# GLA heads six weight blocks apart, v kept in the output's tile, the merge gate in q's and k's, relu and chunk bias on ScalarE

## Chip, cores and metric

One NeuronCore of a Trainium2 chip. The metric is the device time of one execution in microseconds. Before the change: median 1881.58 us of 3 runs (1880.73 to 1882.31).

## The reference, cut to what matters

An encoder block on 256 tokens of 2048 channels in float32: gated linear attention (GLA, 4 heads, both directions) beside a Hyena branch, merged by sigmoid gates, projected, layer norm, then a squared-ReLU MLP and a second norm. The change lies in the GLA part. For each head and direction:

```python
log_a = log_sigmoid(a @ wa2 + ba) / 16            # decay per key channel
b = cumsum(log_a within chunks of 64 tokens)
q_in, k_in = q * exp(b), k * exp(-b)
k_end = k * exp(b[last of chunk] - b)
scores = tril(q_in @ k_in.T)                      # inside a chunk
o = scores @ v + q_in @ state                     # state: sum of k_end.T @ v of earlier chunks, decayed
```

The two directions' outputs are added, normed per head, scaled by a gain and silu(r), and later projected with `w_gla_o`. `sigmoid(g1)`, the first merge gate, then multiplies that projection.

## The kernel before

**Weights.** Every projection is a sequence of blocks of 128 x 2048 floats. `fetch` (L89) loads one block into `raw` (three buffers, SP queue) and splits it in two halves of 1024 columns: ScalarE rounds to `whi` (L81), VectorE takes the remainder to `wlo` (L82); three buffers each. TensorE multiplies high and low parts in separate matmuls and sums in PSUM. A token block (r, v, w_out, the second MLP matrix: `token_products`, L183) has 24 matmuls of 512 columns; a channel block (`channel_pair`, L157: q, k, g1, u, go, ...) has 16 of 512 columns (L142) and 16 of 256 (L146), after which ScalarE copies the low half out (L154) and VectorE adds the high half (L155).

**Order.** `later(d, fn)` (L110) queues a piece of side work; `pump()` (L114) runs once per weight block and calls the pieces that are due d pumps after they were queued; `drain()` calls what is left. The tile scheduler then lays out each engine's instruction order, and puts in the semaphores, from priorities and buffers. Each engine executes its own order strictly in sequence.

**The GLA stage.** The r blocks end with the Hyena filters' last side work, whose results leave by `Td` stores on the POOL queue (L415). Then 16 token blocks for v (four per head) and 16 channel blocks for g1 (two per pair, eight pairs). Beside them, per head h:

- `gla_gates` (L477): z by 4 matmuls (L495); per direction |z| on ScalarE (L499), min(z, 0) on VectorE (L500), Exp and Ln (L501, L502), the difference (L503), a scan per chunk giving b (L508/L510); three exponentials of b: exp(b) (L514), exp(-b) (L515), and for the third the differences to the chunk's last value on VectorE (L518) and their Exp (L520); then products with q and k on VectorE (L522 to L547). b is kept as 16 times the logarithm and the factor 1/16 sits in the exponentials' scale.
- `gla_scores` (L552): score matmuls (L569) from these products, copies, a masked copy, and a split into `sth`, `stl`.
- `gla_out` (L581): 12 matmuls with v (L289 to L291) into two PSUM banks `o`; per bank a square with its sum (L593), the inverse root by Ln and Exp (L212, L213) and small VectorE ops, the product y (L595); then 8 transposes (`yt`, L602) and the split into `yT` (called `yg` in the trace).

For each head the loop (L609) queues gates (0 pumps), scores (3), runs the head's four v blocks, splits the v sums into `vh`, `vl` (high priority, one buffer each), and queues the output (1 pump). Behind the loop `m_sb` (L622) takes two new tiles in the memory of q and k, `channel_pair` writes the g1 sums to them, and at the end of the stage one sigmoid per pair (L636) turns them into the gate. The scheduler may place a sigmoid as soon as its pair is written. Sigmoid and Exp/Ln use different activation tables; a table load is put in wherever ScalarE's order changes from one to the other.

## Time and profile before

| | us |
|---|---|
| median of 3 runs | 1881.58 |
| profiled execution | 1878.99 |
| its span, first to last instruction | 1877.2 |
| TensorE (PE) busy | 1859.6 |
| VectorE (DVE) busy | 1317.7 |
| ScalarE (ACT) busy | 940.8 |
| v blocks, first to last matmul starts | 253.2 to 359.3 |
| g1 blocks | 359.5 to 472.7 |

An engine's busy time counts its instructions from start to end. Matmuls overlap: each row's 0.39 us is longer than the slot it takes in the stream, so costs are read from one start to the next. A row of the timeline has start, duration, engine, line, operation, output<-input, shapes, count, and in brackets the idle time before it with what ended it. A row of waits has the total, the number of times and the longest.

### The profile page before, as it was taken

Reading aid. Unit: us, or ns where it says so; the run is one execution under the profiler, and the core shown is the slowest. Engines: PE = TensorE matmul, PEld = TensorE weight load, DVE = VectorE, ACT = ScalarE, POOL = GpSimd, SP = SyncE. Lnnn points to the kernel's source line nnn. Section 1 sums busy time; section 2 is a strip of 40 time slices with the busy share of each in tenths; the row PEclk is TensorE's granted clock in tenths of the full one; section 3 lists DMA queues with packets and bytes.
Section 4 is the critical chain, followed back from the end, with each engine's and each line's share of the span. In section 5 each row is a group of like instructions: output and inputs, shape, how many; then the busy total and the mean of one; then the engine's idle time right before and its main releaser. Section 6 shows DMA issues by size and latency. Waiting matters only on the chain.

```text
span 1877.2 us, 25196 instructions
## 1 busy us (share of the span) xinstructions
PE 1859.6 (99%) x9948; PEld 1599.3 (85%) x9948; DVE 1317.7 (70%) x1711; ACT 940.8 (50%) x1278; POOL 30.8 (2%) x61
## 2 busy tenths in 40 slices
PE   9999999989999999999999999999999999999998
PEld 7888888878888888888888889888888888888887
DVE  6788878875799999888656667666555655565556
ACT  5555557675555555555544445444434443444332
POOL 1000000000000000000000000000000000000000
PEclk9999999999999999999999999999999999999999
DMA  8567664426555555555555654555555555555553
GB/s 295 208 243 279 227 256 154 180 90 211 185 200 206 197 198 195 201 208 208 213 189 193 259 214 178 201 182 198 182 199 185 199 181 201 187 195 182 199 189 125
DMA packets 60550, 375.07 MB, mean 200 GB/s; under 512 B 6832, under 2 KB 9552, under 8 KB 21008
## 3 DMA queue, kind: packets, MB, share of 16 engines
q1 hardware_dynamic: 47376, 324.03, 48.0%
q0 software_dynamic: 6288, 30.16, 4.3%
q10 hardware_dynamic: 6768, 19.27, 2.8%
q8 instruction: 78, 1.28, 0.3%
q14 instruction: 40, 0.33, 0.0%
HBM read 356.66 MB, written 16.78 MB: 199 GB/s over the span
## 4 chain that ended last, share of the span: by engine, by line
PE 88%; issue 7%; DVE 3%; ACT 1%; DMA 1%; POOL 0%; SPq 0%; DVEq 0%; POOLq 0%; ACTq 0%
PE f L142 12%; PE f L146 7%; PE g L142 6%; PE w L196 6%; PE w L194 6%; PE w L195 6%; PE uz L142 3%; PE ux L142 3%; PE go L142 3%; PE uv L142 3%; PE ho L142 3%; PE g L146 3%; PE ho L146 2%; PE go L146 2%; PE ux L146 2%
## 5 line engine op out<-in xcount | busy, mean ns | idle before, releaser
L82 DVE TENSOR_TENSOR wlo<-raw,whi 128x1024 fp32r<-128x1024 f32 (+2 forms) x603 | 728.6, 1211 | 273.7 <-ACT whi L81 271.0
L81 ACT CAST whi<-raw 128x1024 fp32r<-128x1024 f32 (+2 forms) x603 | 625.0, 1039 | 337.8 <-PE w L196 188.2
L142 PE MATMUL f<-hT,whi 128*128 128x512 f32 (+1 forms) x1048 | 247.6, 387 | 0.0
L142 PEld LDWEIGHTS f<-hT,whi 128*128 128x128 f32 x1048 | 190.9, 189 | 35.5
L195 PE MATMUL w<-wlo,f 128*128 128x512 f32 x480 | 186.7, 389 | 0.0
L196 PE MATMUL w<-whi,f 128*128 128x512 f32 x480 | 186.7, 389 | 0.0
L194 PE MATMUL w<-whi,f 128*128 128x512 f32 x480 | 167.4, 389 | 0.0
L146 PEld LDWEIGHTS f<-hT,wlo 128*128 128x128 f32 x1048 | 134.1, 191 | 4.8
L146 PE MATMUL f<-hT,wlo 128*128 128x256 f32 (+1 forms) x1048 | 135.8, 282 | 0.0
L142 PE MATMUL g<-xT,whi 128*128 128x512 f32 x512 | 124.3, 392 | 3.7 <-DVE vl L82 3.7
L142 PEld LDWEIGHTS g<-xT,whi 128*128 128x128 f32 x512 | 93.7, 188 | 22.1 <-DVE vl L82 4.1
L154 ACT ACTIVATE f_l<-f 128x256 f32<-128x256 f32 x64 | 24.6, 384 | 163.2 <-PE f L142 163.2
L194 PEld LDWEIGHTS w<-whi,f 128*128 128x128 f32 x480 | 90.1, 188 | 18.7
L196 PEld LDWEIGHTS w<-whi,f 128*128 128x128 f32 x480 | 90.1, 188 | 18.7
L195 PEld LDWEIGHTS w<-wlo,f 128*128 128x128 f32 x480 | 90.1, 188 | 18.7
L155 DVE SCALAR_TENSOR_TENSOR f_s<-f,f_l 128x256 f32<-128x256 f32 x64 | 27.2, 425 | 108.8 <-ACT f_l L154 108.7
L146 PEld LDWEIGHTS g<-xT,wlo 128*128 128x128 f32 x512 | 66.0, 191 | 2.6
L146 PE MATMUL g<-xT,wlo 128*128 128x256 f32 x512 | 67.5, 283 | 0.0
L142 PE MATMUL ux<-xT,whi 128*128 128x512 f32 x256 | 64.6, 393 | 0.0
L142 PE MATMUL uz<-xT,whi 128*128 128x512 f32 x256 | 64.5, 393 | 0.0
L142 PE MATMUL go<-yg,whi 128*128 128x512 f32 x256 | 63.6, 392 | 0.0
L142 PE MATMUL uv<-xT,whi 128*128 128x512 f32 x256 | 63.6, 391 | 0.0
(353 smaller groups left out, 3017.5 us busy)
## 6 DMA issues: line engine op xcount, KB each, us to landing
raw<-wblk SPq DMA_DIRECT2D x302, 1024.0 KB, 4.8
Td<-T POOLq DMA_DIRECT2D x16, 768.0 KB, 5.2
Tl<-Td POOLq DMA_DIRECT2D x16, 768.0 KB, 4.6
w<-w4s ACTq DMA_DIRECT2D x16, 512.0 KB, 5.2
zr<-ln_rows ACTq DMA_DIRECT2D x4, 1024.0 KB, 11.1
raw<-wblk SPq DMA_DIRECT2D x11, 256.0 KB, 6.9
dec<-decay_in ACTq DMA_DIRECT2D x8, 256.0 KB, 4.8
yd<-yo POOLq DMA_DIRECT2D x8, 256.0 KB, 4.0
```

The costliest lines, as they stand in the source:

```text
L81: nc.scalar.copy(hi, src)
L82: nc.vector.tensor_tensor(lo, src, hi.bitcast(F32), op=ALU.subtract)
L142: MM(ps[:, :, ts], hi[:, js], act[:, kt, :, ts], start=(kt == 0 and opens), stop=(kt == KT - 1))
L146: MM(ps[:, 0, ts], lo[:, js], act[:, kt, 0, ts], start=False, stop=False)
L154: nc.scalar.activation(low, ps[:, 1], AF.Copy, scale=scale)
L155: nc.vector.scalar_tensor_tensor(dst, ps[:, 0], scale, low, op0=ALU.mult, op1=ALU.add)
L194: MM(pss[tb], sh, wh, start=(kt == 0), stop=False)
L195: MM(pss[tb], sh, wl, start=False, stop=False)
L196: MM(pss[tb], sl, wh, start=False, stop=(kt == KT - 1))
```

## The change

- v: `vh`, `vl` are no tiles of their own. Head h's high and low parts lie in `yT[:, 4h:4h+4]`, the quarter of the output tile that head h's own output is written to later.
- Spacing: all side work of the four heads is queued before the first v block: gates at pump 6h, scores at 6h+4, output at 6h+7 (before: gates at 4h, scores at 4h+3, output at 4h+5).
- Merge gate: `m_sb` is `q_sb` and `k_sb` themselves, no new tiles.
- min(z, 0) on VectorE becomes relu(-(z + bias)/16) on ScalarE, with a bias tile `nba_sb` made once by a 128x16 VectorE op; the difference of L503 becomes a scalar_tensor_tensor that brings in the factor 1/16. b is now the logarithm itself, and exp(b), exp(-b) need no 1/16.
- The third exponential: the VectorE difference over 512 columns and one Exp of 512 become, per direction, six Exps of 64 columns with the chunk's last value of b as per-partition bias. The fourth chunk of each, which nothing reads, is left out.

```diff
+    nba_sb = gp.tile([P, 2, 8], F32, tag="nba", name="nba_sb")
+    nc.vector.tensor_scalar(nba_sb, ba_sb, -1.0 / TAU, None, op0=ALU.mult)
...
                     nc.scalar.activation(a[:, c, :], pzc, AF.Abs, bias=bias)
-                    nc.vector.tensor_scalar(m[:, c, :], pzc, bias, 0.0, op0=ALU.add, op1=ALU.min)
+                    nc.scalar.activation(m[:, c, :], pzc, AF.Relu, scale=-1.0 / TAU,
+                                         bias=nba_sb[:, d, 2 * h + c:2 * h + c + 1])
                 nc.scalar.activation(a, a, AF.Exp, scale=-1.0)
                 nc.scalar.activation(a, a, AF.Ln, bias=ones_sb)
-                nc.vector.tensor_tensor(m, m, a, op=ALU.subtract)
+                nc.vector.scalar_tensor_tensor(m, a, -1.0 / TAU, m, op0=ALU.mult, op1=ALU.subtract)
...
-                nc.scalar.activation(e1, b, AF.Exp, scale=1.0 / TAU)
-                nc.scalar.activation(e2, b, AF.Exp, scale=-1.0 / TAU)
+                nc.scalar.activation(e1, b, AF.Exp)
+                nc.scalar.activation(e2, b, AF.Exp, scale=-1.0)
                 last = 63 if d == 0 else 0
-                b4 = ch4(b)
-                nc.vector.tensor_tensor(
-                    ch4(e3), b4[:, :, :, last:last + 1].broadcast_to([P, 2, 4, 64]), b4, op=ALU.subtract)
-                nc.scalar.activation(e3, e3, AF.Exp, scale=1.0 / TAU)
+                for c in range(2):
+                    for i in ((0, 1, 2) if d == 0 else (1, 2, 3)):
+                        t64 = slice(64 * i, 64 * i + 64)
+                        nc.scalar.activation(e3[:, c, t64], b[:, c, t64], AF.Exp, scale=-1.0,
+                                             bias=b[:, c, 64 * i + last:64 * i + last + 1])
...
     for h in range(HEADS):
-        later(0, gla_gates(h))
-        later(3, gla_scores(h))
-        vh = gp.tile([P, NT, 512], F32R, tag="vh", name=f"vh{h}")
-        vl = gp.tile([P, NT, 512], F32R, tag="vl", name=f"vl{h}")
+        later(6 * h, gla_gates(h))
+        later(6 * h + 4, gla_scores(h))
+        later(6 * h + 7, gla_out(h))
+    for h in range(HEADS):
+        v2 = yT[:, 4 * h:4 * h + 4].rearrange("p k i l -> p (k i l)").rearrange("p (i t d) -> p i t d", i=2, t=NT)
+        vh, vl = v2[:, 0], v2[:, 1]
         pss = token_group(xT, f"v{h}")
...
         v_sb[h] = (vh, vl)
-        later(1, gla_out(h))
...
-    m_sb = [
-        qp.tile([P, 8, L], F32, tag="q", name="m0"),
-        qp.tile([P, 8, L], F32, tag="k", name="m1"),
-    ]
+    m_sb = [q_sb, k_sb]
```

More of the change, by code (lines that the diff above doesn't have):

```diff
@@ L493, in run @@
                     pzc = pz[:, c * L:(c + 1) * L]
-                    bias = ba_sb[:, d, 2 * h + c:2 * h + c + 1]
                     MM(pzc, ws[:, d * L + c * P:d * L + (c + 1) * P], as_sb, start=True, stop=True)
```

## The prediction

> **What bounds the kernel now.** I read the page first, then the busy time by stretches, then what TensorE waited for, then the timeline of the one stretch with a hole in it. From the page:

> ```profile
> span 1877.2 us, 25196 instructions
> PE 1859.6 (99%) x9948; PEld 1599.3 (85%) x9948; DVE 1317.7 (70%) x1711; ACT 940.8 (50%) x1278; POOL 30.8 (2%) x61
> ```

> TensorE is busy in all but 17.6 us of the span, and this change alters none of its matmuls. So only holes in TensorE's stream can be won, and only where the change acts: from the v blocks to the g1 blocks, 253 to 473 us. Busy time by stretches (window, its length, then PE, PEld, DVE, ACT, POOL):

> ```profile
> 282.00:329.00 47.00, 46.74 (x234) 38.77 (x233) 41.15 (x78) 34.23 (x63) 0.00 (x0) 1.00 0.44 152
> 329.00:376.00 47.00, 46.70 (x278) 39.75 (x276) 38.14 (x73) 28.91 (x55) 0.00 (x0) 1.00 0.49 178
> 376.00:423.00 47.00, 41.05 (x244) 35.16 (x245) 33.07 (x74) 35.58 (x66) 0.53 (x1) 1.00 0.26 91
> ```

> The holes are 0.26, 0.30 and 5.95 us: nearly all where head 2's end, head 3 and the last v splits meet. What TensorE waited for (total, times, longest), of its twelve rows those that lie in this stretch:

> ```profile
> PE g L142 <- DVE vl L82: 3.7, 1, 3.7
> PE o L289 <- ACT sth L81: 1.2, 1, 1.2
> PE yt L602 <- DVE y L595: 1.1, 1, 1.1
> PE z L495 <- DVE yg L82: 0.4, 1, 0.4
> ```

> Together 6.4. The largest in the timeline:

> ```profile
> 380.39 0.39 PE L291 MATMUL o<-vh,stl 128*128 128x512 f32 x1
> 384.45 2.11 PE L142 MATMUL g<-xT,whi 128*128 128x512 f32 x8 [3.67 <-DVE vl L82]
> ```

> The reader is to see a chain: v of head 3 could not be split while `vh`/`vl`, one buffer each, still held head 2's v; head 2's output matmuls end at 380.39; only then come the splits that empty v's PSUM banks, which the next gate block needs. The row counts the hole from the modelled end of a 0.39 matmul. Start to start, 4.06 passed where a matmul's slot is about 0.23 (worked out below), so 3.83 was lost: 0.16 more than the row. For four holes that makes 6.4 + 0.6 = **7.0**.

> **The change part by part.**

> *Places and spacing.* v of each head gets its own quarter of `yT`, so its split waits for no earlier head: the 3.83 goes. Scores now come four pumps behind the gates, outputs three behind the scores. In the built kernel's instruction order head 2's score matmuls stand a gate block and more ahead of its output matmuls (before: next to them), and head 3's z matmuls stand later. The 1.2 and the 0.4 go. The merge sums write `q_sb`/`k_sb` pair by pair behind the head that reads that pair: no wait that I can find. All weights, stores and loads keep their order on the SP and POOL queues. From uv on all engines' orders are those of before, but for one f matmul moved by a place; nothing is gained or lost there.

> *VectorE loses* two groups:

> ```profile
> L500 DVE TENSOR_SCALAR gm<-z,ba_sb 128x256 f32<-128x256 f32 x16 | 7.2, 480 | 0.1
> L518 DVE TENSOR_TENSOR e<-gb 128x512 f32<-128x512 f32 x8 | 5.5, 688 | 0.0
> ```

> That is 12.7 us less, over a stretch where it leaves TensorE waiting 0.26 + 0.30. I count half of that, 0.3, as won. One op comes in: the 128x16 scaled bias, which lies in memory that the last filter store still reads:

> ```profile
> 268.63 0.53 POOL L415 DMA_DIRECT2D Td<-T  x1 [10.26 <-DVE T L413]
> 273.22 0.34 ACTq L472 DMA_DIRECT2D scan_sb<-scan_in  x1
> 273.87 1.23 DVE L82 TENSOR_TENSOR wlo<-raw,whi 128x1024 fp32r<-128x1024 f32 x1 [1.50 <-ACT whi L81]
> ```

> The store had landed by 273.22, since the scan load waits for it too. The new op stands ahead of the split at 273.87, where VectorE sat idle 1.50. Cost: nothing. Were the store later, the weight splits behind the op would be late by as much.

> *ScalarE gains* per head four relus, and twelve 64-column exponentials for two of 512. Their prices, from rows where it runs without a gap (each cost is start to next start):

> ```profile
> 377.58 0.84 ACT L499 ACTIVATE ga<-z,ba_sb 128x256 f32<-128x256 f32 x2
> 378.31 1.15 ACT L501 ACTIVATE ga<-ga 128x512 f32<-128x512 f32 x2
> 379.35 1.33 ACT L502 ACTIVATE ga<-ga,ones_sb 128x512 f32<-128x512 f32 x2
> 380.57 0.59 ACT L593 ACTIVATE y<-o 128x512 f32<-128x512 f32 x1
> 381.05 0.20 ACT L593 ACTIVATION_READ_ACCUMULATOR y<-o 128x1 f32 x1
> 381.14 1.07 ACT L81 CAST vh<-v 128x512 fp32r<-128x512 f32 x2
> ...
> 382.67 0.32 ACT L212 ACTIVATE rq_t<-ss,eps_sb 128x1 f32<-128x1 f32 x1
> 382.86 0.65 ACT L514 ACTIVATE e<-gb 128x512 f32<-128x512 f32 x1
> 383.37 0.65 ACT L515 ACTIVATE e<-gb 128x512 f32<-128x512 f32 x1
> ```

> Abs with a per-partition bias, and so a relu: 0.365. Exp 0.52, Ln 0.61, a square with its sum 0.57, one column with such a bias 0.19, the exponentials of b 0.51. No row has 64 columns with a bias. Below it lies the one column, 0.19; above it the 256 columns, 0.365. I take 0.24, near the lower end, as 64 of 256 columns would. That is 4 x 0.365 + 12 x 0.24 - 2 x 0.51 = 3.3 us more per head. In the first two windows ScalarE has 12.8 and 18.1 us to spare, so heads 0 to 2 hide it. I laid those orders out with the same prices, and the tightest split comes some 0.6 ahead of its matmul. Without that cover each 0.1 is a 0.1 lost.

> *Head 3 and the table loads.* The built order has fifteen table loads, before eleven. Head 3's gates now run when the first g1 pair is done, and its sigmoid stands between them: loads for the sigmoid, for Exp, for Ln and for the Exp of head 2's norm come in a row. The price:

> ```profile
> 418.36 0.20 ACT L213 ACTIVATE rq_y<-rq_t 128x1 f32<-128x1 f32 x1
> 418.47 0.37 ACT L154 ACTIVATE g_l<-g 128x256 f32<-128x256 f32 x1
> 418.74 1.04 ACT L81 CAST whi<-raw 128x1024 fp32r<-128x1024 f32 x1
> 419.79 1.28 ACT L636 ACT_TABLE_LOAD   x1
> 421.09 0.63 ACT L636 ACTIVATE m<-m 128x512 f32<-128x512 f32 x1
> 421.62 1.03 ACT L81 CAST whi<-raw 128x1024 fp32r<-128x1024 f32 x1
> 422.56 1.06 ACT L81 CAST yg<-yt 128x512 fp32r<-128x512 f32 x2
> ```

> A weight split costs 0.94 in a row of others, but ahead of a load it is waited out (1.05), and 1.30 later the next starts: a load costs 1.40. Sigmoid 0.53, low half 0.27, one-column Exp 0.11.

> [...]

> Now ScalarE's work from the end of g1's first pair to the high half of block 54 (first half of `g1_2_1`), in the new order: 3 low halves 0.81, 5 splits 4.70, 8 abs/relu 2.92, 4 loads 5.60, sigmoid 0.53, 2 Exp 1.04, 2 Ln 1.22, 2 squares 1.14, 2 + 2 one-column 0.60, 4 exponentials 2.06, 12 short ones 2.88: **23.5**, with 0.3 for start and last tail 23.8. TensorE's work in the same stretch: 4 z, 3 blocks, 12 output matmuls, 2 transposes (0.11 each, an estimate from the narrow ones):

> ```profile
> 424.42 2.08 PE L146 MATMUL g<-xT,wlo 128*128 128x256 f32 x16
> 426.33 3.82 PE L142 MATMUL g<-xT,whi 128*128 128x512 f32 x16
> 429.99 2.08 PE L146 MATMUL g<-xT,wlo 128*128 128x256 f32 x16
> ```

> Sixteen wide matmuls take 3.66 (0.23 each), sixteen narrow ones 1.91 (0.12): a block 5.57. So 0.48 + 16.71 + 2.76 + 0.22 = 20.2. In this order ScalarE never waits there, so TensorE does: 23.8 - 20.2 = **3.6 lost**. VectorE's path to the transpose just ahead (exponentials, products, then y) I put at about 23, so it hides under the same wait. Bounds of the short exponentials: at 0.19 each 0.6 less, at 0.365 each 1.5 more.

> *The last output (head 3).* Its two norms still pay four loads in series. Before, a split and a low half (0.94 + 0.27) stood between them, and the transpose waited 1.1; in the new order both stand elsewhere. The wait goes; it is the most doubtful of the 7.0.

> **Sum:** -7.0 - 0.3 + 3.6 = -3.7; I take -3.6, since the holes left never vanish quite. The profiled execution took 1878.99 us, its span 1877.2 and 1.8 around it, so 1875.4 by that. It lies 2.6 below the median of the runs, 1881.58; against the median the forecast is **1878.0 us**, 0.19% faster. A measurement of this kernel tells about 0.2%, 3.8 us, from no change, so my forecast stands on that line.

> **Rivals.**

> *The whole gain.* If the loads find cover (ScalarE ahead of my count by 3 us), all 7.3 are won: 1874.3. For it: ScalarE is half idle on the page. Against: the in-order sum above has no idle place. 0.15.

> *The wait moves.* ScalarE in head 3 is 2 us later than I count, or heads 0 to 2 lose their 0.6 margins and the last transpose keeps its 1.1: 3 more lost, 1881.0. For it: VectorE is taken for 41.15 of 47 us while heads 0 and 1 run, and in head 3 every late ScalarE op is on the path. Against: 12.7 us less on VectorE. 0.17.

> *Each switch of tables drains ScalarE.* If a load kept the engine for twice its 1.28, the four in head 3 would cost 5.1 more: 1883.1. Against: sigmoid starts 0.02 behind the load's end at 419.79 + 1.28. 0.03. [...]

> *Slower.* The 64-column exponentials do not overlap and cost as much as a whole 256-column row with bias, some 0.48 (L499's 0.84 for two less one slot of 0.365). Then 12 x 0.24 = 2.9 more per head: head 3 loses 2.9 more, heads 0 to 2 each 2.9 less about 1 of margin, 5.7. That is 8.6 against 3.6 won: 1886.6. From about 0.38 each the sign turns. Against: behind the one-column row the next starts after 0.19. With anything like it, 0.10.

> *It does not do what it says:* v's splits still wait for another head through the shared tile. Then 3.8 comes back: 1881.8. The built order shows v's splits waiting for their matmuls alone. 0.02.

> **How the numbers follow.** Forecast 0.53, its spread of 1876 to 1880 lying a little more than half on the near side of 3.8 us: 0.30 faster, 0.23 the same. With the whole gain's 0.15, faster 0.45. With the moved wait's 0.17, the drain's 0.03 and 0.02 for nothing done, the same 0.45. Slower 0.10. The range runs from the whole gain, 1874.3, to the moved wait with the dear bound of the short exponentials, 1881.0 + 1.5: 1874.2 to 1882.5. The slower rival and the drain stay outside.

> **What would show it.** Right: no wait of g on vl; three or four more table loads in the g1 stage; short exponentials 0.24 apart; a hole of 3 to 4 us in TensorE at `g1_2`, some 140 us behind the first v matmul, ending on a split, a y or a weight half. Wrong: a hole in heads 0 to 2, a wait of v's split on an output, loads over 1.4, or any change behind 480 us.

## The result and the profile after

The changed kernel takes **1876.27 us** (median of 7 executions, 1874.85 to 1876.94) against 1881.63 (7, 1880.73 to 1882.55) for the kernel before: ratio 0.997, 95% interval 0.996 to 0.998, so 5.4 us or 0.28% less. Forecast were 1878.0 and a range of 1874.2 to 1882.5. The profiled execution took 1875.42; the forecast for it was 1875.4.

The page of the changed kernel, the two lines that answer to those of before:

```profile
span 1873.6 us, 25223 instructions
PE 1858.0 (99%) x9948; PEld 1598.3 (85%) x9948; DVE 1307.2 (70%) x1688; ACT 959.0 (51%) x1338; POOL 30.8 (2%) x61
```

VectorE lost 10.5 us of busy time and ScalarE gained 18.2; neither says what became of the time. The same three stretches do (window, its length, PE, PEld, DVE, ACT, POOL, PEclk, DMA share, GB/s):

```profile
282.00:329.00 47.00, 47.00 (x236) 39.31 (x235) 38.25 (x73) 40.35 (x92) 0.00 (x0) 1.00 0.45 162
329.00:376.00 47.00, 47.00 (x282) 40.48 (x281) 35.18 (x66) 33.47 (x74) 0.00 (x0) 1.00 0.42 154
376.00:423.00 47.00, 44.18 (x261) 38.08 (x260) 30.20 (x56) 37.13 (x73) 0.00 (x0) 0.96 0.39 143
```

TensorE has no gap while heads 0 to 2 run. The third stretch still has 2.82 us of hole, and a column that was 1.00 before reads 0.96: the clock. What TensorE waited for, the rows of this stage (total, times, longest; of the second row's 1.6, 0.63 lies here, the other 1.0 further on):

```profile
PE yt L606 <- DVE rq_t L216: 2.0, 1, 2.0
PE g L146 <- DVE wlo L82: 1.6, 2, 1.0
PE g L142 <- ACT whi L81: 0.2, 1, 0.2
PE yt L606 <- DVE y L599: 0.2, 1, 0.2
```

The waits on `vl`, on `sth` and on `yg` are gone; the last transposes' wait fell from 1.1 to 0.2. New are the first three rows. They lie together in TensorE's timeline:

```profile
390.44 1.11 PE L146 MATMUL g<-xT,wlo 128*128 128x256 f32 x8
392.18 1.22 PE L146 MATMUL g<-xT,wlo 128*128 128x256 f32 x8 [0.63 <-DVE wlo L82]
393.24 2.00 PE L142 MATMUL g<-xT,whi 128*128 128x512 f32 x8
397.20 0.66 PE L606 MATMUL yt<-ident,y 128*128 128x128 f32 x2 [1.96 <-DVE rq_t L216]
398.09 3.29 PE L142 MATMUL g<-xT,whi 128*128 128x512 f32 x8 [0.23 <-ACT whi L81]
401.22 0.33 PE L573 MATMUL s<-qi,kk 128*128 128x64 f32 x2
```

Start to start, less a slot each, the three lose 0.79, 2.13 and 0.67: 3.59. The eight wide matmuls behind them take 3.13 (398.09 to 401.22) where eight at full rate take 1.83 (half of the 3.66 of sixteen in the prediction's rows): 1.30 more. The granted clock (PEclk, third from the end) says why:

```profile
396.00:397.00 1.00, 0.00 (x0) 0.00 (x0) 1.00 (x3) 1.00 (x5) 0.00 (x0) 1.00 0.22 90
397.00:398.00 1.00, 0.66 (x2) 0.26 (x2) 1.00 (x6) 1.00 (x3) 0.00 (x0) 0.63 0.00 0
398.00:399.00 1.00, 0.91 (x2) 0.81 (x3) 1.00 (x3) 1.00 (x3) 0.00 (x0) 0.50 0.00 0
399.00:400.00 1.00, 1.00 (x4) 0.71 (x4) 1.00 (x3) 1.00 (x3) 0.00 (x0) 0.50 0.00 0
400.00:401.00 1.00, 1.00 (x5) 0.82 (x4) 1.00 (x2) 0.98 (x3) 0.00 (x0) 0.66 0.11 25
```

Behind the hole TensorE ran at half rate, a granted clock of 0.50, for 3.41 us (397.27 to 400.68). Its clock had stayed at 1.00 behind the 3.83 hole of the kernel before, in that profile.

Why the holes are there is on ScalarE, in the same stretch:

```profile
381.51 1.28 ACT L504 ACT_TABLE_LOAD   x1
382.81 1.15 ACT L504 ACTIVATE ga<-ga 128x512 f32<-128x512 f32 x2
...
392.74 1.53 ACT L523 ACTIVATE e<-gb 128x64 f32<-128x64 f32 x6
394.18 0.19 ACT L213 ACTIVATE rq_y<-rq_t 128x1 f32<-128x1 f32 x1
...
397.00 1.03 ACT L81 CAST whi<-raw 128x1024 fp32r<-128x1024 f32 x1
397.94 0.30 ACT L545 COPY qx<-qi 128x128 f32<-128x128 f32 x1
```

From the end of the first g1 pair, 374.36, to this split's end at 398.03 ScalarE runs without a gap, four table loads among it: 23.7 us. One early sigmoid brings four loads, not two: behind its own, Exp (381.51), Ln and Exp again each have one. In the kernel before, Exp and Ln stand here one behind the other without a load (378.31 and 379.35 in the prediction's rows), and so they do in run 2. Why the built program loads between Exp and Ln only behind a sigmoid no run here shows.

Length of the stage by the profiles, first v matmul to first uv matmul: 219.33 before, 216.24 after, 3.09 less. What lies ahead of it took 0.41 less, what lies behind 0.1 less.

### The profile page after: what moved, and what is told of

Read it like the earlier page. It is cut to its first block, busy times and chain, and to the rows that moved or that the text cites. A ratio compares the mean times of both kernels' runs of the same rounds, so it can differ in the third digit from the quotient of the medians.

```text
span 1873.6 us, 25223 instructions
## 1 busy us (share of the span) xinstructions
PE 1858.0 (99%) x9948; PEld 1598.3 (85%) x9948; DVE 1307.2 (70%) x1688; ACT 959.0 (51%) x1338; POOL 30.8 (2%) x61
## 3 DMA queue, kind: packets, MB, share of 16 engines
q8 instruction: 78, 1.28, 0.3%
## 4 chain that ended last, share of the span: by engine, by line
PE 90%; issue 4%; ACT 2%; DMA 2%; DVE 1%; SPq 0%; POOL 0%; DVEq 0%; POOLq 0%; ACTq 0%
PE f L142 12%; PE f L146 7%; PE w L195 6%; PE w L194 6%; PE w L196 6%; PE g L142 4%; PE uv L142 3%; PE ho L142 3%; PE ux L142 3%; PE uz L142 3%; PE g L146 2%; PE go L142 2%; PE ho L146 2%; PE uv L146 2%; PE r L195 2%
## 5 line engine op out<-in xcount | busy, mean ns | idle before, releaser
L82 DVE TENSOR_TENSOR wlo<-raw,whi 128x1024 fp32r<-128x1024 f32 (+2 forms) x603 | 727.7, 1210 | 283.6 <-ACT whi L81 278.8
L81 ACT CAST whi<-raw 128x1024 fp32r<-128x1024 f32 (+2 forms) x603 | 625.7, 1039 | 346.5 <-PE w L196 188.2
L142 PE MATMUL f<-hT,whi 128*128 128x512 f32 (+1 forms) x1048 | 246.7, 386 | 0.0
L142 PEld LDWEIGHTS f<-hT,whi 128*128 128x128 f32 x1048 | 190.0, 188 | 35.5
L146 PEld LDWEIGHTS f<-hT,wlo 128*128 128x128 f32 x1048 | 134.1, 191 | 4.8
L146 PE MATMUL f<-hT,wlo 128*128 128x256 f32 (+1 forms) x1048 | 135.8, 282 | 0.0
L142 PE MATMUL g<-xT,whi 128*128 128x512 f32 x512 | 125.9, 395 | 0.2 <-ACT whi L81 0.2
L142 PEld LDWEIGHTS g<-xT,whi 128*128 128x128 f32 x512 | 94.5, 190 | 18.7 <-ACT whi L81 0.6
L154 ACT ACTIVATE f_l<-f 128x256 f32<-128x256 f32 x64 | 24.5, 384 | 162.9 <-PE f L142 162.9
L146 PEld LDWEIGHTS g<-xT,wlo 128*128 128x128 f32 x512 | 66.1, 191 | 4.5 <-DVE wlo L82 2.1
L146 PE MATMUL g<-xT,wlo 128*128 128x256 f32 x512 | 68.1, 284 | 1.6 <-DVE wlo L82 1.6
L142 PE MATMUL ux<-xT,whi 128*128 128x512 f32 x256 | 64.6, 393 | 0.0
L142 PE MATMUL uz<-xT,whi 128*128 128x512 f32 x256 | 64.5, 393 | 0.0
L142 PE MATMUL go<-yg,whi 128*128 128x512 f32 x256 | 63.6, 392 | 0.0
L142 PE MATMUL uv<-xT,whi 128*128 128x512 f32 x256 | 63.6, 391 | 0.0
```

Of the source, the lines that this page charges most:

```text
L81: nc.scalar.copy(hi, src)
L82: nc.vector.tensor_tensor(lo, src, hi.bitcast(F32), op=ALU.subtract)
L142: MM(ps[:, :, ts], hi[:, js], act[:, kt, :, ts], start=(kt == 0 and opens), stop=(kt == KT - 1))
L146: MM(ps[:, 0, ts], lo[:, js], act[:, kt, 0, ts], start=False, stop=False)
L154: nc.scalar.activation(low, ps[:, 1], AF.Copy, scale=scale)
```

## The experiments

Theory: two memories bind TensorE behind head 3's v blocks, v's and that of the merge sums, and the change frees both; the sums' sigmoids then come early, and their table loads put ScalarE's in-order work late, which costs half of it again. Rival: the gate edits' relief of VectorE, or the spacing, makes the gain. In the table, "v" is v in `yT`, "m" the sums over q and k, "late" sigmoids issued behind the stage, each in the `go` block that uses it; "stage" is first v to first uv matmul in the run's profile. Ratios are to the kernel before on the same chip, with 95% intervals.

| run | v | m | late | gate edits | spacing | table loads | stage, us | median, us | ratio |
|---|---|---|---|---|---|---|---|---|---|
| 1 before again | | | | | | 11 | 220.84 | 1881.68 | 0.9998 (0.9989 to 1.0007) |
| 7 | | | | x | | 11 | 218.01 | 1880.30 | 0.9995 (0.9986 to 1.0004) |
| 9 | | | x | | | 6 | 219.54 | 1879.36 | 0.9986 (0.9977 to 0.9996) |
| 3 | x | | | | | 11 | 220.05 | 1880.13 | 0.9990 (0.9981 to 0.9999) |
| 10 | | x | | | | 19 | 223.99 | 1884.10 | 1.0013 (1.0004 to 1.0022) |
| 8 | x | x | | | x | 19 | 223.62 | 1883.52 | 1.0008 (0.9999 to 1.0016) |
| 5 | x | | | x | x | 11 | 216.44 | 1876.38 | 0.9973 (0.9963 to 0.9983) |
| 11 the change | x | x | | x | x | 15 | 216.68 | 1875.86 | 0.9971 (0.9959 to 0.9983) |
| 2 | x | x | x | x | x | 6 | 212.87 | 1872.92 | 0.9954 (0.9942 to 0.9967) |
| 4 | x | x | x | | x | 6 | 211.35 | 1872.97 | 0.9953 (0.9939 to 0.9966) |
| 6 | x | x | x | x | | 6 | 212.01 | 1872.74 | 0.9956 (0.9943 to 0.9969) |
| 12 | x | x | x | | | 6 | 211.62 | 1871.33 | 0.9945 (0.9932 to 0.9959) |

**Run 1**, the kernel before without an edit.

> The kernel before, unchanged, profiled once more. Clock theory: after a hole of some 4 us TensorE's clock is halved for about 3.4 us in most executions; the first profile missed it, and that is why it lies 2.6 us under the median. Then this profile shows a granted clock near 0.5 right behind the hole at 384 us and a time near 1881, or, where the clock stays at 1.00 there, a time near 1879 again. Rival: the 2.6 us are from elsewhere (start, DMA); then clock at the hole and time of the execution do not go together.

The times agree, but this profiled execution is 2.6 us longer than the first, 1.5 of it in the stage (220.84 against 219.33). The clock there differs (same columns as above):

```profile
379.00:380.00 1.00, 1.00 (x5) 0.76 (x4) 1.00 (x3) 1.00 (x3) 0.00 (x0) 0.62 0.06 16
380.00:381.00 1.00, 1.00 (x4) 0.81 (x3) 0.17 (x2) 1.00 (x3) 0.00 (x0) 0.50 0.00 0
...
386.00:387.00 1.00, 1.00 (x4) 0.76 (x4) 1.00 (x4) 1.00 (x4) 0.00 (x0) 0.53 0.00 0
387.00:388.00 1.00, 1.00 (x4) 0.81 (x3) 1.00 (x4) 1.00 (x5) 0.00 (x0) 0.50 0.00 0
```

The same kernel now has two half-rate stretches of 3.4 us here. The first lies over head 2's output matmuls and costs nothing, since the wait for `vl` ends it all: from the first of them to the g block 6.72 us pass (378.54 to 385.26), as in the first profile (377.73 to 384.45). The second lies on the g block and does cost.

So the end of those matmuls does not set the g block's start by itself: here the last of them starts 2.37 us later than in the first profile (382.76 against 380.39), the g block only 0.81. VectorE's order has its part in it. In the first profile the split `vl` stands behind head 3's gate work (VectorE's timeline):

```profile
380.10 1.30 DVE L503 TENSOR_TENSOR gm<-gm,ga 128x512 f32<-128x512 f32 x2 [0.83 <-ACT ga L502]
381.32 1.27 DVE L508 TENSOR_TENSOR_SCAN gb<-scan_sb,gm 128x256 f32<-128x256 f32 x2
382.50 0.13 DVE L214 TENSOR_SCALAR rq_v<-ss 128x1 f32<-128x1 f32 x1
382.54 1.27 DVE L510 TENSOR_TENSOR_SCAN gb<-scan_sb,gm 128x256 f32<-128x256 f32 x2
383.72 0.67 DVE L82 TENSOR_TENSOR vl<-v,vh 128x512 fp32r<-128x512 f32 x1
```

**Run 2**, the changed kernel; the eight sigmoids moved out of the stage, each into the `go` block that uses its gate.

```
-    for c2 in range(8):
-        mp = m_pair(c2)
-        nc.scalar.activation(mp, mp, AF.Sigmoid)
...
+        tc.keep_in_program_order(nc.scalar.activation(mp, mp, AF.Sigmoid))
```

> The changed kernel, but each sigmoid of the merge gate is issued in the projection block that uses it, pinned there: no table load between Exp and Ln is left in the g1 stage (15 loads become 6). Theory (ScalarE's queue in head 3, with four loads, makes the holes): its 23.8 us of work shrink by 5.6 + 0.5 to 17.7 against 20.2 of TensorE, the holes at g1_1 and g1_2 (0.8 + 2.1 + 0.7) and the half clock behind them (1.3) go: some 4.9 less than the changed kernel, about 1871.4. Rival (VectorE's products set the holes, whatever the loads): 1875 to 1876, holes still there.

All waits of head 3 are gone, no half-rate stretch lies in the stage, and the time falls by some 3 us more (1872.92 against 1876.27 and, in run 11, 1875.86). So the sigmoids' early place made the change's hole. Of the work that it brings, the loads are the large part (four, against one sigmoid of 0.53), and the theory's second half holds.

**Run 3**, the kernel before with v in `yT` alone.

```
-        vh = gp.tile([P, NT, 512], F32R, tag="vh", name=f"vh{h}")
-        vl = gp.tile([P, NT, 512], F32R, tag="vl", name=f"vl{h}")
+        v2 = yT[:, 4 * h:4 * h + 4].rearrange("p k i l -> p (k i l)").rearrange("p (i t d) -> p i t d", i=2, t=NT)
+        vh, vl = v2[:, 0], v2[:, 1]
```

> The kernel before with one part of the change alone: v in yT's quarters; spacing, merge gate and gates as before. Theory (the single v buffer was the large hole): the hole of 3.8 us goes, the waits of o on sth (1.3), z on yg (0.5) and yt on y (1.2) stay: some 3.8 less than before, up to 5.6 with the half clock gone: 1876 to 1878. Rival (VectorE's 12.7 us less work made the gain): within 1 us of before, with another wait in the place of the hole.

A miss: 0.1% instead of 0.2 to 0.3%. The hole only changed its reason (TensorE's timeline):

```profile
389.38 2.00 PE L142 MATMUL g<-xT,whi 128*128 128x512 f32 x8
395.88 3.25 PE L142 MATMUL g<-xT,whi 128*128 128x512 f32 x8 [4.51 <-DVE m L155]
```

The block waits for the first merge sum, `m`, whose tile is q's memory and comes free only when head 3's gates have read all of q. The waits on `sth` and `yg` went with v's place alone.

**Run 4**, as run 2 without the gate edits (VectorE's minimum and chunk difference as before).

> The changed kernel without its edits in the gates (min, difference and chunk difference on VectorE as before, exponentials of 512 columns), with the sigmoids late as in the run above. Theory (the gain is v's place and the spacing; the gate edits only move 3.3 us per head to a ScalarE that without loads has room, and 3 us per head from a VectorE that is loaded but hidden): within 1.5 us of the run above, about 1871 to 1873. Rival (VectorE relief is needed once heads are spaced): 1875 or more, with TensorE waiting on wlo or y.

The same time as run 2, so the gate edits add nothing once the sigmoids are late. TensorE is busy in the whole stage; its 211.35 us are the floor, and the kernel before lost 219.33 - 211.35 = 8.0 in it.

**Run 5**, the changed kernel with the sums in new tiles again.

```
-    m_sb = [q_sb, k_sb]
+    m_sb = [
+        qp.tile([P, 8, L], F32, tag="q", name="m0"),
+        qp.tile([P, 8, L], F32, tag="k", name="m1"),
+    ]
```

> The changed kernel with one part undone: the merge gate's sums m go into new tiles in the memory of q and k again, not over q and k in place. A new tile is released only when head 3's gates have read all of q, so no sum can be written while they run; the sigmoids then also come behind the gates, and only 11 table loads are left instead of 15. Theory (each part takes away another reason of the same hole; with v in place the next reason is this one): TensorE's weight block for g waits for the sums as in the run with v alone (4.5 there), 3 to 6 us in one hole behind head 3's scores, and the holes of the change on a weight half and on the transposes (0.6 and 2.0) are gone; time within 2 us of the changed kernel's, 1874.5 to 1878.5. Rival A (the merge gate's place is worth nothing, and only the table loads made the change's hole): no wait for m, and about the time with the sigmoids last, 1872 to 1873.5. Rival B (the place is worth more than the loads cost): over 1879.

As the theory had it, but for a hole a little under its 3 us:

```profile
392.29 2.64 PE L142 MATMUL g<-xT,whi 128*128 128x512 f32 x8 [2.67 <-DVE m L155]
```

The late sums hold the sigmoids back (11 loads), and the time is that of the change: sums in place bring as much as their early sigmoids cost.

**Run 6**, as run 2 with the old due times.

```
-        later(6 * h, gla_gates(h))
-        later(6 * h + 4, gla_scores(h))
-        later(6 * h + 7, gla_out(h))
+        later(0, gla_gates(h))
+        later(3, gla_scores(h))
...
+        later(1, gla_out(h))
```

> The changed kernel with the sigmoids issued behind head 3's heads (as in the second run), and the old spacing: gates, scores and head outputs issued with each v block's own due times (0, 3 and 1 pumps later) instead of six weight blocks per head. v and the merge gate stay in place, and the gate edits stay. If places alone did it: as with the new spacing, 1872 to 1873.5, no wait inside the stage from v to g. My theory: the spacing is worth the short holes: head 3's scores and its output stand one behind the other with 5 weight groups between, so a wait for the scores' eviction (1.2 before) and one for y (1.1 before) come back, 1 to 3 us in all: 1873.5 to 1876.

My theory missed: the time is run 2's. The spacing adds nothing once the two places are free.

**Run 7**, the kernel before with the gate edits alone (the diff's first three hunks).

> The kernel before with the gate edits alone (relu as ScalarE activation, the scaled subtraction, the chunk bias in 64-column Exps; 11 table loads as before). Theory (TensorE's holes come from the memory of v and of the merge gate, and VectorE's relief is hidden): within 1.5 us of the kernel before, the wait for vl still there at 2 to 5 us. By the prediction's own sum VectorE would give 0.3 and ScalarE's 3.3 per head could lengthen the waits behind head 3 by up to 3. Rival (VectorE's relief of some 12 us is what made the gain): 4 us or more faster than before.

```profile
381.69 2.12 PE L142 MATMUL g<-xT,whi 128*128 128x512 f32 x8 [2.89 <-DVE vl L82]
```

The wait on `vl` stands, and the time is that of before within 0.14%. VectorE's relief did not make the gain.

**Run 8**, the changed kernel without the gate edits.

> The changed kernel without the gate edits (VectorE takes the minimum and the chunk difference as before; v, merge gate and spacing as in the change; the sigmoids not moved). 19 table loads stand in the program instead of 15. Theory (ScalarE's order of work in head 3 is late, and the loads are what makes it late): four loads of 1.30 to 1.40 more and 3.3 of gate work less per head; if the extra loads stand inside head 3's stretch the hole is up to 2 us longer, if only two do it is about as long: 1875 to 1879, and a hole that ends on ScalarE's work is still there. Rival (the gate edits' 3.3 us on ScalarE is what makes it late): no hole, 1872 to 1873.5 as in the fourth run.

Slower than forecast, and slower than every other arrangement with v in place:

```profile
391.80 1.11 PE L146 MATMUL g<-xT,wlo 128*128 128x256 f32 x8
402.26 3.78 PE L142 MATMUL g<-xT,whi 128*128 128x512 f32 x8 [9.35 <-ACT whi L81]
```

ScalarE's table loads between 374 and 404 us, by line (count, busy us, mean ns):

```profile
L634 ACT ACT_TABLE_LOAD x2 | 2.6, 1283 | 0.0
L514 ACT ACT_TABLE_LOAD x2 | 2.6, 1283 | 0.0
L212 ACT ACT_TABLE_LOAD x2 | 2.6, 1283 | 0.0
L501 ACT ACT_TABLE_LOAD x1 | 1.3, 1283 | 0.0
L502 ACT ACT_TABLE_LOAD x1 | 1.3, 1283 | 0.0
L520 ACT ACT_TABLE_LOAD x1 | 1.3, 1283 | 0.0
```

Eight of these nine stand ahead of the weight half that TensorE waits for; in the changed kernel four do. The gates' exponentials (L514, L520) alternate with the norm's logarithm (L212). In the change all of a head's exponentials depend on b alone, and the ScalarE program runs them in one set behind both logarithms; without it the last waits for VectorE's difference, and the norm's logarithm comes between (that this wait is why the order differs is inferred). So the gate edits are worth 7 us inside the change (ratio 1.0008 against 0.9971 in run 11 on the same chip), against their own 3.3 us per head on ScalarE. By runs 2 and 4, where no such loads are left and the time is the same with and without them, it is not VectorE's time but the four table loads; some 2.5 us of it is half rate behind the hole (half of the 5.06 from 402.26 to 407.32, see the last section).

**Run 9**, the kernel before with the sigmoids late (run 2's diff).

> The kernel before with the sigmoids alone issued behind head 3's heads (6 table loads instead of 11; v, merge gate, spacing and gate edits as before). Theory (v's own memory is what TensorE waits for behind head 3's output, and the sums' own tiles behind that; table loads only decide once both are in place): the wait for vl stays at 2 to 4 us, only the wait for y (1.1) can go: 1879 to 1881.5, within 2 us of before. Rival (the late sigmoids alone are what made the second and the fourth run fast): 1873 to 1876.

```profile
384.41 2.97 PE L142 MATMUL g<-xT,whi 128*128 128x512 f32 x8 [2.11 <-DVE vl L82]
```

As the theory had it: the wait for y is gone, that on `vl` stays (2.11 behind output matmuls at half rate, as in run 1).

**Run 10**, the kernel before with the sums in place alone (`m_sb = [q_sb, k_sb]`).

> The kernel before with the merge gate's sums over q and k in place, alone (v in its own tiles, old spacing, gates and sigmoids as before). 19 table loads stand in the program, as in the run without the gate edits, because the first sums no longer wait for head 3's gates and their sigmoids are put between the gate's Exp, Ln and Sqrt. Theory (each load is 1.30 to 1.40 of ScalarE's order, and the place frees nothing as long as v's tiles bind): slower than before by 0 to 5 us, 1881 to 1886.5, with a wait of several us on ScalarE's weight half or on y behind head 3. Rival (the place by itself gives the gain): 1878 or less.

Slower by 0.13%, as expected. Among its waits (TensorE's timeline):

```profile
395.62 1.22 PE L146 MATMUL g<-xT,wlo 128*128 128x256 f32 x8 [0.93 <-DVE wlo L82]
...
401.02 3.14 PE L142 MATMUL g<-xT,whi 128*128 128x512 f32 x8 [2.34 <-ACT whi L81]
```

Late weight halves, and no wait on `vl` any more, though v has its own tiles: g blocks run on in front of and behind head 2's output matmuls, and the last `vl` splits start only at 397.45 with nobody waiting for them. Early sums by themselves fetch early loads, and these cost more than the waits that went.

**Run 11**, the changed kernel once more.

> The changed kernel unchanged, for a second profile and more executions. Theory (a hole draws half-rate stretches of TensorE's clock in some executions and not in others; each costs about 1.7 us): median 1875.3 to 1877.3, mean granted clock near 0.999 against 0.997 of before; in the profile the same holes of 0.6, 2.0 and some 0.2 in head 3, and behind them a half-rate stretch of 3.4 us or none; by this the profiled time is 1874 to 1877. Rival (the half rate of the first profile belongs to the change's hole and comes every time): again from 397 to 401 us.

The same holes (0.64, 1.96 and 0.46), and behind them half rate again, from 399.9 to 403.4 us. In both profiles of the change the stretch is there, so by these two the rival stands: the hole draws it. For before it came in one of two. Nor has any of the 15 executions of the change a mean clock of 1.000, as seven of the 20 of runs 2, 4, 6 and 12 have.

**Run 12**, the kernel before with both places and late sigmoids, and nothing else (the diffs of runs 3, 10 and 2).

> The kernel before with three edits only: v lies where the head's output will go, the merge gate's sums lie over q and k, and the sigmoids are issued behind head 3's heads. Spacing and gate edits as before; 6 table loads. Theory (two memories bound TensorE behind head 3, and the table loads of sigmoids that come early took the gain back; spacing and gate edits add nothing to this): 1872 to 1874, no wait of over 1 us in the stage from v to g, no half-rate stretch in it. Rival (spacing and gate edits stand in for each other, and one of the two is needed): a wait of 1 to 4 us behind head 3's scores or heads, 1875 to 1879.

```profile
282.00:329.00 47.00, 47.00 (x236) 39.31 (x235) 42.27 (x80) 34.49 (x64) 0.00 (x0) 1.00 0.45 162
329.00:376.00 47.00, 47.00 (x280) 40.38 (x279) 39.46 (x77) 30.63 (x59) 0.00 (x0) 1.00 0.47 168
376.00:423.00 47.00, 47.00 (x287) 41.17 (x286) 35.23 (x72) 29.59 (x59) 0.08 (x1) 1.00 0.38 135
```

The best of all by its median, and 0.55% faster than before; its interval overlaps those of runs 2, 4 and 6. TensorE has no hole, with VectorE at 42.27 of 47 us. Two memories and one place in ScalarE's program are enough for the whole gain. That the sums' place is needed run 5 shows, by its wait for `m` with v in place. For v's place it is not shown: no run has the sums in place and the sigmoids late with v in its own tiles, and in run 10 the wait on `vl` went without it.

## Why the prediction was right, and where it was not

- *v's place, 3.83, and the small waits:* right for the change; all four rows of before are gone or at 0.2. The chain behind the 3.83 was read too simply: the buffer held the split back, but VectorE's gate work ahead of it in order, until 383.72, ended the wait (run 1). The credit was shared out wrongly. The 1.2 and the 0.4 went with v's place alone (run 3), not with the spacing (run 6). And v's place without the sums' place wins only 0.1% (run 3), while with the sums' place alone the waits on `vl`, `sth` and `yg` go too (run 10).
- *The size of what could be won:* the prediction counted 7.0 + 0.3; by the floor of run 4 it was 8.0.
- *VectorE's relief, 0.3:* the 0.26 and 0.30 were indeed won, but run 12 wins them with VectorE as busy as before. The reason failed, at a small price.
- *ScalarE's prices:* the abs/relu rows start 0.36 apart (0.365 taken), six short exponentials take 394.18 - 392.74 = 1.44, 0.24 each, as taken. Heads 0 to 2 hide them. The slower rival, which had them at 0.48, fell with that.
- *Head 3 and the loads:* ScalarE's 23.8 came out at 23.7, the loss of 3.6 at 3.59, and runs 2 and 8 point to the loads as its cause. VectorE's path, put at about 23, ended with y at 397.14, 22.8 behind the same start: it ends the largest hole, and ScalarE's split the next, 0.67 later. The two paths end within 0.9 us of each other, so one hides under the other, as put. A load costs 1.30 to the next start (381.51 to 382.81). The rival that drains ScalarE at each switch fell: the Exp starts 0.02 behind that load's end (381.51 + 1.28).
- *What the sum left out:* the clock. The prediction took it as 1.00 behind the hole, since before's profile had it so. It cost 1.30. Stage: -8.0 + 3.59 + 1.30 = -3.1, as measured (-3.09). That the profiled time was still met (1875.42 against 1875.4) is luck: 0.7 more to win than counted, and 0.5 less ahead of and behind the stage, made up for the 1.30.
- *The step to the median failed:* the prediction carried over the 2.6 us by which before's profiled execution lay under the median. After, it is 0.85. That is the 1.7 between 1878.0 and 1876.27. Run 1 and the clocks below suggest why: the first profile of before was one with few half-rate stretches.
- *The whole gain, 0.15:* needs the loads out of the way, not cover for them. Run 2 does this, at 1872.92.

## What to carry to other kernels

When a wait on memory goes, list what its end had held back: here early sums let sigmoids in among the gates, and each switch of tables cost 1.30 us on the engine that splits the weights. Count the table loads of the built program between two points of the bound engine, and put activations of another set that are not urgent behind them. And before carrying a profile's numbers to a median, see which of its slow stretches the profiled execution happened to have.

## What the runs showed of the hardware

```profile
397.00:398.00 1.00, 0.00 (x0) 0.00 (x0) 0.76 (x1) 0.99 (x2) 0.00 (x0) 0.54 0.00 0
...
407.00:408.00 1.00, 1.00 (x7) 0.91 (x7) 0.29 (x1) 0.12 (x1) 0.00 (x0) 0.84 1.06 451
```

That is from 397.1 to 407.3, 10.2 us. One on a busy TensorE costs half of 3.4, 1.7: an estimate from that length and the granted 0.50. A gap of 2.0, with one of 0.6 ahead of it, was followed by half rate in both profiles of the change, 3.7 in the first profile of before and 2.9 in run 7 by none. Of the ten profiles with a hole of 1.9 us or more in this stage eight had half rate there, of the four without such a hole none. In the profiles with more than one stretch their starts lie on a grid of that length. Run 1 has a third stretch, from 1164.30: 778.24 us behind the second's start at 386.06, 228 times 3.4133. In the change's profile a second one starts at 1871.82, 1474.56 behind the first at 397.27, 432 times 3.4133. Cut this stage in each profile along the grid that its own stretches give, and add up TensorE's idle time in each cell of 3.41 us: ten of the 13 half-rate cells follow one with 1.96 us idle or more, and no cell without half rate behind it has over 1.94 (run 7). The 3.67 of the first profile of before fell into two cells, 1.82 and 1.85; the 2.0 of the change lay in one. In the change, then, half rate followed a cell with 1.96 of its 3.41 idle. The other three follow less (1.53 in runs 1 and 9, and 1.76 in run 8, a cell that was itself at half rate), so idle time alone does not tell all of it, and no run moved the grid on purpose.

TensorE kept to its order where later work was ready: in the change's profile it stands idle 0.63 ahead of the narrow matmuls at 392.18, while the `whi` half of the eight wide ones behind them (393.24) was split by 390.09 (ScalarE, L81, 389.05 + 1.04).

The mean granted clock was 0.9973 over the 88 executions of the kernel before that were measured beside these runs and 0.9987 over 15 of the changed one, so 5.1 and 2.4 us of clock were missing (0.0027 of 1878, 0.0013 of 1874), 3.0 and 1.4 stretches' worth at 1.7. The first profile of before held one such stretch, run 1's three. Before, the 9 executions at 0.999 took 1880.4 on average, the 46 at 0.997 took 1882.3. The 1.6 stretches that the change has fewer are worth up to 2.7 us, and less where they lie on a wait. That the 1.8 us by which the medians differ more than the profiles come from them is inferred from this, not shown by a run of its own.
